# Padded rows in the raw tiles and state transfers in four pieces: a one-core RWKV kernel

## Chip, cores and metric

One Trainium2 chip; the kernel runs on 1 of its cores. The metric is the device time of one execution in microseconds, lower is better. The time before is a median of 317.09 us over 3 runs (315.88 to 317.64).

## What is computed

The WKV recurrence of RWKV over k and v of shape (16, 2048, 256), float32, with a decay vector w and a bonus vector u of 256 numbers. Each of the 16 x 256 channels carries three numbers (aa, bb, pp) through 2048 steps:

```python
for b in range(batch):
    aa, bb, pp = 0, 0, -1e38                 # vectors of d_model
    for t in range(seq_len):
        kk, vv = k[b, t, :], v[b, t, :]
        ww = u + kk
        qq = np.maximum(pp, ww)
        e1, e2 = np.exp(pp - qq), np.exp(ww - qq)
        output[b, t, :] = (e1 * aa + e2 * vv) / (e1 * bb + e2 + 1e-08)
        ww = pp - w + kk
        qq = np.maximum(ww, kk)
        e1, e2 = np.exp(ww - qq), np.exp(kk - qq)
        aa, bb, pp = e1 * aa + e2 * vv, e1 * bb + e2, qq
```

## The kernel before

**Tiles and stages.** Time is cut into 16 chunks of 128 steps, and each chunk into 4 tiles of 4 batches, so there are 64 tiles n; tile n belongs to chunk c = n // 4. A raw tile of k or v holds 128 time steps on the partitions and 4 batches x 256 channels behind each other (512 KB, 4 KB per partition). `load_k` and `load_v` (L91 to L102) fetch them: those of the first two tiles are issued on SP's queue, the other 124 on POOL's, where issuing is work of POOL itself (the rows L94 and L101). In HBM the four rows of 1 KB of one partition lie far apart, in the raw tile they lie side by side.

**One tile's way.** `round_k` (L184) rounds k to float32r, three of four tiles on DVE and the fourth on POOL; `cast_v` (L204) turns v into bfloat16, the first nine tiles on DVE, later ones on POOL. Twice per tile, PE forms sums of k over time in PSUM (`rows`, L191, and `logs`, L197), and ACT takes their exponentials into the ring EZR (`exps`, L200), which has room for 12 tiles. DVE multiplies them by v (`times_v`, L209), and PE sums (`sums`, L235). Ten tiles later the output is made: PE applies triangular matrices to EZR for the denominator (`den`, the name DEN) and the numerator (`num`, the name NUM), both in `apply` (L319); ACT takes logarithm and inverse (L337, L341); DVE multiplies (`mult`, L349) into one of five output buffers `ot`, and SP stores it in three DMAs (L355 and twice L358).

**State.** After the fourth tile of a chunk the state of all channels is carried on: sums are copied and turned (L241, L248), a chain of small DVE and ACT steps (L252 to L290) gives the state at the chunk's start, PE turns it back (`turn_back`, L294), DVE copies it to the 128 x 128 tile `cb` (L298), and `inject` (L305) writes it by DMA into EZR. There, rows 63 and 127 of EZR (each half chunk's last row) take the state, in place of the exponentials that stood there. DEN and NUM of the chunk's four tiles wait for this transfer ("IN"). The last chunk does without it.

**Order.** Every engine runs its instructions in the order of the program. That order is made when the program is built: each operation has a place (the table P, in units of a tile), operations are sorted by place, and the first whose predecessors are done and whose buffers are free is issued next (L409 to L439). The buffer counts stand in one line:

```python
NK, NKP, NV, NVB, NRD, NOT = 3, 5, 6, 2, 2, 5
```

`kf` has 5 buffers (NKP), `vr` 6 (NV; it also holds k of the first two tiles), `ot` 5 (NOT). SP's queue holds the state transfers and the stores, in program order; a transfer that waits for `cb` holds up the stores behind it. In each round of 4 tiles SP issues 2 state DMAs and 12 store DMAs. `zeros` (L135) issues matmuls that fill idle time of PE and change nothing.

Of the kernel before, what the change touches and what calls it, by code (L numbers as in the profile page):

```python
# [7 lines left out]
F32 = mybir.dt.float32  # L8
# [7 lines left out]
def kernel(  # L16
# [9 lines left out]
    K = tc.keep_in_program_order  # L26
    PE, DVE, SC, POOL, SP = nc.tensor, nc.vector, nc.scalar, nc.gpsimd, nc.sync

    B, T, Dm = k.shape
    HS = 64  # L30
    TC = 2 * HS
    NST = T // TC
    D = 2 * Dm
# [3 lines left out]
    BYSP = 2  # L37
    EARLY = 9
    PLAN = "DDDP"
# [2 lines left out]
    CAP = 54.0  # L42
    BIG = 1e30
    MM = 15
    FILL = 1
    P = {"LK": -5.73, "LV": -3.92, "RK": [-1.335, -1.2, -1.16, -1.575], "L": [-11.28, -6.145],
         "X": [-7.455, -4.505], "CV": [-0.72, -1.04, -0.995, -4.145], "TV": [1.435, 2.275, 2.29, 2.405],
# [10 lines left out]
    kppool = ctx.enter_context(tc.tile_pool(name="kppool", bufs=NKP))  # L58
    vpool = ctx.enter_context(tc.tile_pool(name="vpool", bufs=NV))
# [22 lines left out]
    def rows_of(x, n):  # L82
        c, p = divmod(n, 4)
        return x[4 * p:4 * p + 4, c * TC:(c + 1) * TC, :].rearrange("n t d -> t n d")

    KR, VR, VB = {}, {}, {}

    def how(n):
        return "D" if n < BYSP else PLAN[n % len(PLAN)]

    def load_k(n):  # L91
        if how(n) != "C":
            KR[n] = (vpool if n < BYSP else kppool).tile([128, 4, Dm], F32, tag="vr" if n < BYSP else "kf", name="kf")
            K((SP if n < BYSP else POOL).dma_start(out=KR[n], in_=rows_of(k, n)))  # L94
        else:
            KR[n] = kpool.tile([128, 4, Dm], F32R, tag="kr", name="kr")
            K(POOL.dma_start(out=KR[n], in_=rows_of(k, n)))

    def load_v(n):
        vr = vpool.tile([128, 4, Dm], F32, tag="vr", name="vr")  # L100
        K((SP if n < BYSP else POOL).dma_start(out=vr, in_=rows_of(v, n)))  # L101
        VR[n] = vr  # L102

# [5 lines left out]

    K(DVE.memset(WUf, 0.0))  # L110
    load_k(0)
    row_wu(w, 0)
    row_wu(u, 1)
# [19 lines left out]
    def zeros(m, first=False):  # L133
        for j in range(m):
            K(PE.matmul(TOT[:, 256:448], Z[:, 0:128], Z, start=first, stop=True, skip_group_check=True))  # L135
# [38 lines left out]
    EZR = consts.tile([128, 4, RING, 2, D], BF16, tag="EZR", name="EZR")  # L174
# [7 lines left out]
    def round_k(n):  # L182
        kr = kpool.tile([128, 4, Dm], F32R, tag="kr", name="kr")
        K((DVE if how(n) == "D" else POOL).tensor_copy(kr, KR[n]))  # L184
        KR[n] = kr
# [95 lines left out]
    def state_spread(c):  # L281
        CB, G = CB_of[c % 2], G_of[c % 2]
        x = AB[:, :, :, 0:2].rearrange("p a (b m) h -> p a h b m", b=4)
        y = G[:, 2, :, 1:3].rearrange("p (b m) h -> p h b m", b=4).unsqueeze(1).broadcast_to([128, 2, 2, 4, 8])
        if c >= MM:
            x, y = (z.rearrange("p a h b m -> p h a b m") for z in (x, y))
# [14 lines left out]
    def inject(c):  # L301
        cb = st.pop((c, "cb"))
        r0 = 4 * c % RING
        for q in (1, 0):
            K(SP.dma_start(out=EZR[HS - 1::HS, 2 * (1 - q), r0:r0 + 4, :, :].rearrange("h p i (b x) -> h (p i b) x", b=4),  # L305
                           in_=cb[HS * q:HS * q + HS, :]))


    RD, NUM, OT = {}, {}, {}
# [1 line left out]
    def apply(out_tile, n, names, q0):  # L311
        c, p = divmod(n, 4)
        if c >= MM:
            names = ({"L": "S", "LN": "SN"}[names[0]], names[1])
        for s in range(2):
            for i in range(2):
                for h in range(2):
# [3 lines left out]
                                tile_position=(r, o), skip_group_check=True))  # L321
        if c >= MM:
            for b in range(4):
# [40 lines left out]
    def step(name, place, fn, args=(), after=(), take=None, give=(), mode=0):  # L364
        ops[name] = dict(place=place, fn=fn, args=args, after=list(after), take=take, give=give, mode=mode)

    for n in range(NP):
# [4 lines left out]
        tail = n >= NP - LAG  # L372
        place = lambda key: m + (P["TAIL"][key] + (n - NP + LAG) * P["TAIL"]["step"] if tail else P["OUT"][key][j])
        kb = "V" if early else "KP" if how(n) != "C" else "K"
        if n:
            step(("LK", n), n + P["LK"], load_k, (n,), [("LK", n - 1)], kb)
        else:
            free["V"] -= 1
        step(("LV", n), n + P["LV"], load_v, (n,), [("LV", n - 1)] + ([("LK", n)] if n else []), "V")
        if how(n) != "C":  # L380
            step(("RK", n), put("RK"), round_k, (n,), [("LK", n), ("RK", n - 1)], "K", [kb])
# [8 lines left out]
        if j == 3:  # L390
            s = P["STATE"][0 if c == 0 else 2 if c == NST - 1 else 1]
            for i, (name, fn, *after) in enumerate((
                    ("CS", copy_sums, ("S", n)), ("TU", turn, ("CS", c), ("CH", c - 1)), ("SL", state_logs, ("TU", c)),
                    ("FR", state_frames, ("SL", c), ("SN", c - 1)), ("OF", state_offsets, ("FR", c)),
                    ("SW", state_weights, ("OF", c)), ("CH", state_chain, ("SW", c), ("KP", c - 1)),
                    ("SS", state_spread, ("CH", c)), ("TK", turn_back, ("SS", c), "mats"), ("BK", copy_back, ("TK", c)),
                    ("IN", inject, ("BK", c)), ("SN", state_next, ("OF", c)), ("KP", state_keep, ("CH", c)))):
                if not (name in ("SN", "KP") and c + 1 == NST or name == "IN" and c >= MM):
                    step((name, c), n + s[i], fn, (c,), after, mode=1)
# [12 lines left out]
    while todo:  # L412
        for name in todo:
            o = ops[name]
# [13 lines left out]
        if o["give"] == ["X"]:  # L428
            x = held[("DEN", name[1]) if name[0] == "LN" else ("R",) + name[1:]]
# [5 lines left out]
        if o["mode"] and not quiet:  # L435
            zeros(P["Z0" if name[-1] < FILL else "Z"].get(name[0], 0))
        quiet = quiet and name[0] != "CS" or name[0] == "S" and name[1] % 4 == 3
# [32 lines left out]
```

## Time and profile before

| | |
|---|---|
| median of 3 runs | 317.09 us |
| profiled execution | 316.14 us |
| its span, first to last instruction | 314.4 us |
| mean granted TensorE clock | 0.971 |
| HBM read, written | 67.12 MB, 33.55 MB |
| L200 exponentials, ACT | 128 of 1.01 us |
| L337 and L341, ACT | 64 of 1.02 us and 64 of 1.06 us |
| L349 output multiplication, DVE | 64 of 1.22 us |
| L184 rounding of k | 48 of 0.73 us on DVE, 16 of 1.04 us on POOL |
| L204 cast of v | 9 of 0.73 us on DVE, 55 of 1.28 us on POOL |
| L94, L101 issue of a load, POOL | 62 of 0.76 us, 62 of 0.78 us |
| a load from issue to landing | 7.8 us (k), 8.1 us (v), median |

Busy shares are averages over the span, over stages with different limits. Idle time of an engine counts only where that engine, or one that waits for it, sets the end. The time of a load's issue on POOL is not the time of its transfer: the transfer runs on the 16 DMA engines, which all queues share. A packet record of the trace is one piece of a transfer on one DMA engine, with its queue (q0: issued by POOL; q1: issued by SP), start, duration and size.

### The profile page before, as it was taken

The page shows a single profiled execution, that of the slowest core. Times are in us where ns is not written, and L with a number is a line of the kernel's source. Part 1 is how long each engine was busy: PE and PEld are TensorE (multiplying, and loading weights), DVE is VectorE, ACT ScalarE, POOL GpSimd, SP SyncE. Part 2 cuts the span into 40 slices and gives each one's busy share as a digit, 9 for nine tenths or more (in the row PEclk, how much of TensorE's full clock was granted, in tenths as well). Part 3 has the DMA queues.
Part 4 walks back from the last instruction along what each step waited for, and adds up shares of the span by engine and source line. Part 5 has one row for each costly group of instructions (what it writes and reads, how often), then busy time and mean ns, then how long its engine had stood idle before and what let it go on. Part 6 is the DMA issues. An engine that isn't in the chain of part 4 may idle for free.

```text
span 314.4 us, 7474 instructions
## 1 busy us (share of the span) xinstructions
PE 275.7 (88%) x2927; PEld 127.2 (40%) x2927; DVE 242.9 (77%) x430; ACT 259.1 (82%) x289; POOL 181.7 (58%) x213
## 2 busy tenths in 40 slices
PE   7898977999998998999897999799998979987840
PEld 7444742444343443444343434334443434432430
DVE  5879874588887879898878688787887866898650
ACT  1585554999999998999897999789998977997960
POOL 8855582385868585777848486846767552510000
PEclk9999997999999999999999999989999998999995
DMA  7999999889999999999999999999999996636986
GB/s 233 353 347 347 350 346 323 253 247 344 315 354 380 378 377 353 384 374 389 346 394 371 384 345 371 383 356 358 331 391 361 394 321 226 176 98 182 270 252 176
DMA packets 57840, 101.67 MB, mean 323 GB/s; under 512 B 7108, under 2 KB 41932, under 8 KB 57804
## 3 DMA queue, kind: packets, MB, share of 16 engines
q0 software_dynamic: 17856, 65.02, 59.0%
q1 hardware_dynamic: 39932, 36.16, 35.9%
q8 instruction: 23, 0.38, 0.5%
q14 instruction: 13, 0.11, 0.1%
q10 hardware_dynamic: 16, 0.01, 0.0%
HBM read 67.12 MB, written 33.55 MB: 320 GB/s over the span
## 4 chain that ended last, share of the span: by engine, by line
DMA 41%; PE 26%; ACT 12%; DVE 11%; issue 4%; SPq 3%; DVEq 0%; ACTq 0%
DMA out_dram<-ot 33%; ACT EZR L200 7%; DVE ot L349 7%; PE X L197 6%; DMA EZR<-cb 6%; PE TOT L135 5%; PE X L191 4%; PE num L319 3%; PE X L319 3%; ACT rd L337 3%; SPq L358 2%; PE TOT L235 2%; DMA WUf<-in_u_dram 2%; ACT rd L341 2%; DVE EZR L209 1%
## 5 line engine op out<-in xcount | busy, mean ns | idle before, releaser
L200 ACT ACTIVATE EZR<-X 128x1024 bf16<-128x1024 f32 x128 | 125.2, 1014 | 21.1 <-PE X L197 21.1
L349 DVE TENSOR_TENSOR ot<-num,rd 128x1024 f32<-128x1024 f32 x64 | 78.0, 1219 | 28.6 <-DMA out_dram<-ot 8.2
L94 POOL DMA_DIRECT2D kf<-in_k_dram x62 | 47.1, 760 | 72.3 <-DVE kr L184 66.3
L204 POOL CAST vb<-vr 128x1024 bf16<-128x1024 f32 x55 | 70.2, 1277 | 21.1 <-DVE EZR L209 19.0
L209 DVE TENSOR_TENSOR EZR<-EZR,vb 128x2048 bf16<-128x2048 bf16 x64 | 79.6, 1262 | 0.9 <-ACT EZR L200 0.9
L337 ACT ACTIVATE rd<-X 128x1024 f32<-128x1024 f32 x64 | 65.4, 1023 | 12.5 <-PE X L319 12.1
L341 ACT ACTIVATE rd<-rd 128x1024 f32<-128x1024 f32 x64 | 67.8, 1059 | 2.0
L135 PE MATMUL TOT<-Z 128*128 128x192 bf16 x367 | 64.8, 261 | 2.2 <-DVE Z L119 1.6
L191 PE MATMUL X<-WU,CO 64*64 64x512 bf16 x512 | 53.4, 406 | 1.8 <-DVE WU L166 0.9
L135 PEld LDWEIGHTS <-Z 128*128 128x128 bf16 x367 | 33.8, 102 | 50.5 <-issue 48.4
L101 POOL DMA_DIRECT2D vr<-in_v_dram x62 | 48.3, 779 | 2.1 <-DMA vr<-in_v_dram 1.8
L197 PE MATMUL X<-kr,NLE 128*128 128x512 f32 x128 | 46.9, 448 | 0.0
L197 PE MATMUL X<-kr,NLZ 128*128 128x512 f32 x128 | 46.2, 442 | 0.0
L184 DVE CAST kr<-kf 128x1024 fp32r<-128x1024 f32 x48 | 35.1, 732 | 1.7 <-PE X L197 0.9
L319 PE MATMUL num<-EZR,LN 64*64 64x512 bf16 x240 | 25.0, 406 | 12.3 <-DVE ot L349 9.2
L319 PE MATMUL X<-EZR,L 64*64 64x512 bf16 x240 | 24.8, 401 | 8.6 <-DMA EZR<-cb 6.6
L191 PEld LDWEIGHTS <-CO 64*64 64x64 bf16 x512 | 15.9, 104 | 37.8 <-issue 35.8
L319 PE MATMUL num<-EZR,IdN 64*64 64x512 bf16 x256 | 25.7, 384 | 0.0
L319 PE MATMUL X<-EZR,Id 64*64 64x512 bf16 x256 | 25.6, 380 | 0.0
L235 PE MATMUL TOT<-EZR,OH 128*32 128x256 bf16 x512 | 24.0, 281 | 0.9 <-DVE EZR L209 0.8
L298 DVE CAST cb<-TURN 128x128 bf16<-128x128 f32 x16 | 4.7, 291 | 22.6 <-PE TURN L294 22.6
L319 PEld LDWEIGHTS <-LN 64*64 64x64 bf16 x240 | 8.3, 104 | 34.0 <-issue 25.6
(70 smaller groups left out, 215.9 us busy)
## 6 DMA issues: line engine op xcount, KB each, us to landing
kf<-in_k_dram POOLq DMA_DIRECT2D x62, 512.0 KB, 7.8
vr<-in_v_dram POOLq DMA_DIRECT2D x62, 512.0 KB, 8.1
out_dram<-ot SPq DMA_DIRECT2D x64, 256.0 KB
out_dram<-ot SPq DMA_DIRECT2D x128, 128.0 KB
kf<-in_k_dram SPq DMA_DIRECT2D x2, 512.0 KB
vr<-in_v_dram SPq DMA_DIRECT2D x2, 512.0 KB
EZR<-cb SPq DMA_DIRECT2D x30, 16.0 KB
WUf<-in_w_dram ACTq DMA_DIRECT2D x1, 4.0 KB
```

The lines of the kernel that those rows point to most:

```text
L94: K((SP if n < BYSP else POOL).dma_start(out=KR[n], in_=rows_of(k, n)))
L101: K((SP if n < BYSP else POOL).dma_start(out=vr, in_=rows_of(v, n)))
L135: K(PE.matmul(TOT[:, 256:448], Z[:, 0:128], Z, start=first, stop=True, skip_group_check=True))
L191: K(PE.matmul(X[a][o:o + HS, i, :].rearrange("p (n d) -> p n d", n=2), CO[r:r + HS, q, :], WU[r:r + HS, :].unsqueeze(1).broadcast_to([HS, ...
L197: K(PE.matmul(X[a][:, i, :], (NLE, NLZ)[q], km[:, i, :], start=False, stop=True, skip_group_check=True))
L200: K(SC.activation(ez(n)[:, q], X[a], ACT.Exp))
L204: K((DVE if n < EARLY else POOL).tensor_copy(vb, VR.pop(n)))
L209: K(DVE.tensor_mul(ez(n)[:, 2:4], ez(n)[:, 0:2], vb.unsqueeze(1).broadcast_to([128, 2, 2, D])))
L319: K(PE.matmul(out_tile[o:o + HS, i, :], mats[names[s]][r:r + HS, r:r + HS], ez(n)[r:r + HS, q0 + s, i, :], start=s == 0, stop=s == 1, tile ...
L337: K(SC.activation(rd, X[a], ACT.Ln, scale=RS))
L341: K(SC.activation(RD[n], RD[n], ACT.Exp, scale=-1.0))
L349: K(DVE.tensor_mul(o.rearrange("p (i n) d -> p i (n d)", i=2), NUM.pop(n), RD.pop(n)))
```

## The change

Two edits. First, `raw` allocates the raw tiles of k and v with 8 more floats (32 B) behind each row of 256 and hands out the view without them, so that the rows of a partition stand 1056 B apart instead of 1024. The rounding and the cast read through that view. Second, a state transfer is issued as four DMAs instead of two. Before, each wrote 32 rows of `cb` (256 B each) into partition 63 and 32 into partition 127; now each piece moves 32 rows of `cb` into one partition, 8 KB in one run there. The order of the halves q stays. `CF` is 0, so `how` gives what it gave.

```diff
+    CF = 0
+    PAD = 8
...
     def how(n):
-        return "D" if n < BYSP else PLAN[n % len(PLAN)]
+        return "D" if n < BYSP else "C" if n < CF else PLAN[n % len(PLAN)]
+
+    def raw(pool, tag):
+        return pool.tile([128, 4, Dm + PAD], F32, tag=tag, name=tag)[:, :, 0:Dm]
 
     def load_k(n):
         if how(n) != "C":
-            KR[n] = (vpool if n < BYSP else kppool).tile([128, 4, Dm], F32, tag="vr" if n < BYSP else "kf", name="kf")
+            KR[n] = raw(vpool, "vr") if n < BYSP else raw(kppool, "kf")
             K((SP if n < BYSP else POOL).dma_start(out=KR[n], in_=rows_of(k, n)))
...
     def load_v(n):
-        vr = vpool.tile([128, 4, Dm], F32, tag="vr", name="vr")
+        vr = raw(vpool, "vr")
         K((SP if n < BYSP else POOL).dma_start(out=vr, in_=rows_of(v, n)))
...
         for q in (1, 0):
-            K(SP.dma_start(out=EZR[HS - 1::HS, 2 * (1 - q), r0:r0 + 4, :, :].rearrange("h p i (b x) -> h (p i b) x", b=4),
-                           in_=cb[HS * q:HS * q + HS, :]))
+            for h in range(2):
+                r, x = HS * h + HS - 1, 32 * (2 * q + h)
+                K(SP.dma_start(
+                    out=EZR[r:r + 1, 2 * (1 - q), r0:r0 + 4, :, :].rearrange("o p i (b x) -> o (p i b) x", b=4),
+                    in_=cb[x:x + 32, :]))
```

## The prediction

> **What bounds the kernel now.** I read the page first (busy shares, slices, queues), then the table by stage, the list of waits, the queue's own waits, and the timeline around the longest waits. All sums are made against the profiled execution: 316.14 us, of which 314.4 us are the span, so 1.7 us lie around it. The median of the runs shown is 317.09 us, 0.95 us above it.
>
> ```profile
> PE 275.7 (88%) x2927; PEld 127.2 (40%) x2927; DVE 242.9 (77%) x430; ACT 259.1 (82%) x289; POOL 181.7 (58%) x213
> ...
> q0 software_dynamic: 17856, 65.02, 59.0%
> q1 hardware_dynamic: 39932, 36.16, 35.9%
> ```
>
> The two DMA queues together hold the 16 engines for 95% of the span. PE's share contains idle-filling matmuls (L135, 64.8 us), so ACT, not PE, is the fullest compute engine. The table by stage shows when this holds (columns: PE, PEld, DVE, ACT, POOL busy us of 15, granted clock, DMA share, GB/s):
>
> ```profile
> 45.00:60.00 15.00, 10.51 (x100) 4.32 (x99) 7.01 (x16) 8.40 (x10) 7.00 (x9) 0.89 0.99 314
> ...
> 105.00:120.00 15.00, 13.26 (x148) 5.72 (x143) 11.32 (x20) 14.32 (x16) 10.60 (x12) 1.00 1.04 373
> 120.00:135.00 15.00, 14.88 (x158) 6.63 (x151) 12.85 (x21) 14.04 (x16) 9.94 (x11) 1.00 1.04 380
> ...
> 270.00:285.00 15.00, 13.30 (x163) 5.57 (x163) 13.17 (x23) 13.89 (x16) 4.98 (x4) 1.00 0.55 161
> ```
>
> From 75 to 255 us ACT is busy 12.0 to 14.6 of 15 us, mostly over 14, and the DMA engines are full at once: two limits of nearly the same height. Over those twelve rows ACT is idle 11.3 us. From 45 to 60 us ACT loses 6.6 us at one place:
>
> ```profile
> 39.34 1.24 SPq L305 DMA_DIRECT2D EZR<-cb  x2
> ...
> 49.36 0.41 PE L319 MATMUL X<-EZR,L 64*64 64x512 bf16 x4 [4.36 <-DMA EZR<-cb]
> ...
> 50.04 1.02 ACT L337 ACTIVATE rd<-X 128x1024 f32<-128x1024 f32 x1 [5.30 <-PE X L319]
> ```
>
> The first state transfer needs 10.0 us from its issue until DEN(0) may read it. PE has nothing else in its order from 45.0 us on, and ACT stands behind PE. The other waits that the change can touch:
>
> ```profile
> POOL kf L94 <- DVE kr L184: 66.3, 37, 6.7
> ...
> ACT rd L337 <- PE X L319: 12.1, 14, 5.3
> ...
> DVE ot L349 <- DMA out_dram<-ot: 8.2, 5, 2.5
> PE X L319 <- DMA EZR<-cb: 6.6, 4, 4.4
> ...
> PE num L319 <- DMA EZR<-cb: 2.4, 2, 1.4
> ```
>
> The first line is slack: loads wait for a free k buffer, and between 85 and 255 us a k tile lands 11 to 16 us before its rounding starts. Stores have no slack: DVE waits for an output buffer that a store holds, and SP itself is held, since the trace shows its 226 DMAs using eight completion semaphores in turn, each issue waiting for the landing of the eighth DMA before it:
>
> ```profile
> SPq L358 <- DMA out_dram<-ot: 18.3, 25, 1.6
> ```
>
> **Why the transfer is slow.** The trace's packet records tell it. Queue q1 closes its DMAs with 4 B packets: 3196 = 196 x 16 + 30 x 2, so every load and store runs on 16 engines and each state transfer on two. Loads on q0 move in packets of 4096 B, 192 ns each while only loads run, 172 to 188 ns beside stores. Between 43.8 and 47.9 us each of the two engines sends one 256 B packet (18 ns), then one 4096 B packet, every 207 ns: strict turns. The two transfers queue 64 such packets on each of those engines. At 267.8 us, with no load running, the first packet starts 1.19 us after the issue and the last 2.33 us; in the first transfer these are 4.47 and 9.25 us.
>
> **Part 1, four pieces of 32 rows.** It adds 30 SP issues of 0.6 us (L305, two in 1.2 us). If a piece spreads over 16 engines, an engine gets 2 packets of each piece, 8 per state instead of 64. The last piece is issued 3 x 0.62 = 1.9 us after the first, at 41.2 us. With the same 4.47 us to the first packet, two turns of 0.21 and the 0.8 us that lay between last packet and PE, it lands near 46.9 us: 2.5 us gained. The upper end is the whole 4.36 us of PE's wait, since DEN(0) can't start before 45.0. I take 3.5, because part 2 should shorten the turns too. Of the later waits on EZR<-cb (6.6 + 2.4 - 4.36 = 4.6 us) and ACT's one long wait behind them (2.53 us at 205 us) I take 2.5, bounds 0 and 4.6.
>
> What it costs: after each transfer twelve stores stand behind it on SP and start 1.2 us later, and the pieces take four of the eight semaphores instead of two. Stores already leave 6 to 10 us after their multiplication, and OT has five buffers, so this is hidden except where an output buffer is waited for: 5 waits x 1.2 = 6 us at most, nothing at least. I take 1.
>
> The Trainium skill, "DMA: Bandwidth & Descriptors", section on why a DMA increments its semaphore by 16, says that the engine count is the largest number up to 16 that divides the slowest dimension above 1 on both sides. Two destination rows give two engines there, as the 30 x 2 closing packets agree, and 32 rows against 32 would give 16. By it the piece spreads as assumed.
>
> **Part 2, the padding.** The destination of one partition's four rows is no longer one run of 4096 B. If packets follow runs, q0 goes from 15,872 packets of 4096 B to 63,488 of 1024 B. Price per KB: q1's 1 KB packets take 46 to 47 ns as stores beside loads; SP's four opening loads, the same shape in 1 KB packets, take 46 to 51, and move 350 GB/s from 5.4 to 8.4 us, against 346 GB/s for the 4096 B packets that follow. So the load-bound start (8 to 40 us) loses nothing. Beside stores a KB costs 43 to 47 ns now (172/4 to 188/4); 44 to 46 is +8 us of DMA time over the load phase (63,488 x 2 ns / 16), and 44 to 51 is +28. Cover: the 11 to 16 us of lead of the loads, and, on the two engines that carry the state now, the loss of 960 state packets each (960 x 18 ns = 17 us). I take 0, bounds -4 and +14 (28 less 14).
>
> The gain is in the turns. A tile's stores are 32 packets per engine: with a load packet between each, 32 x (46 + 176) = 7.1 us now, 32 x (46 + 48) = 3.0 us after. Stores land 8 us after issue on average and held DVE for 8.2 us. Bounds 0 and 8.2; I take 2, since ACT's idle time in those rows is shared with part 1's 2.5 and some 0.26 us per state step remains anyway.
>
> L94 and L101 on POOL (124 x 0.77 us): four times the destination runs. No row has a POOL issue of another shape; SP issues 512-packet loads in 0.45 to 0.51 us and 128-packet stores in 0.62, no growth with count. Bounds 0 and a doubling (+95 us of POOL, 277 of 314). I take 0. The casts (L184, L204) read rows with a gap; the elements stay side by side within 256. Nearest dearer row: DVE's one element per cycle in L349, 1219 against 732 ns, 57 x 0.49 = 28 us more DVE, mostly under ACT. I take 0, bounds 0 and +8.
>
> A rule against this part: the Trainium skill, "DMA: Bandwidth & Descriptors", section on how a descriptor splits into AXI transactions, has 256 B lines, and a run that starts off such a line pays for the part before it. Rows at +0, +32, +64, +96 B would then cost 32 to 35 beats instead of 32, an estimate of 5% on the loads, 0.05 x 184 = 9 us of DMA time. No row here shows an unaligned run.
>
> **Sum.** -3.5 - 2.5 + 1 - 2 = -7.0 us: span 307.4, profiled time 309.1, median 310.0 us.
>
> **Rivals.**
> 1. *The padding does not change the packets.* For: POOL's issue already names 1024 B elements, and packets may be filled to 4096 B whatever the runs. Then only part 1 acts: -2.5 - 2 + 1 = -3.5, 313.5 us.
> 2. *Slower: the finer packets overfill the DMA engines.* Place: 75 to 255 us. With 1.50 us of stores (512 x 47 / 16) and a share of 1.04, a tile fits ACT's 4.27 us (2 x 1.01 + 1.02 + 1.06, and a quarter of 0.28 + 0.36) as long as a load packet costs under 46 ns (1024 x 46 / 16 = 2.94; 4.44 / 1.04 = 4.27). At 51 ns a tile takes 4.58, 0.31 over, x 42 tiles = 13 us; at 53, 0.43 x 42 = 18. The lead of 12 us hides part, but stores now hold half the turns and loads come late first: PE X L197 then waits for kr. Net +3 to +14, 320 to 331; I put it at 325. For: the shares of 1.04. Against: the 350 GB/s of the opening loads.
> 3. *Slower: POOL's issue grows* to 1.5 us or more, delaying casts and loads: some 335.
> 4. *The pieces do not spread*, all 128 rows on one engine: 128 turns of 0.21 instead of 64, or stores held by the semaphores: +2 to +6, 321.
> 5. *The wait moves*: PE's freed time is given back at the output buffers: 316 to 317.5.
>
> **How the numbers follow.** Forecast 41%, rival 1 20%, rival 5 10%, rival 2 16%, rival 3 6%, rival 4 7%. About 0.5% (1.6 us) is what a measurement of this kernel can tell from no change. Faster: 0.41 x 0.95 + 0.20 x 0.85 = 0.56; slower: 0.29 from rivals 2 to 4 plus 0.02 of the others; same: the rest, 0.13. The forecast's own range is 304 to 315. Reaching out to most of rivals 2 and 4 gives 303 to 324, with about 5% below and 14% above.
>
> **What would show it.** Right: q0 with about 65,000 packets; closing packets of state pieces 16 each; EZR<-cb landing within 7 us of the first issue and PE's 4.36 us wait under 2; store landings shorter and DVE ot's wait on out_dram under 4 us; POOL's issue still near 0.75 us, the casts near 732 and 1277 ns. Wrong: q0 with 17,856 packets (rival 1); DVE kr or PE X waiting for DMA kf (rival 2); POOL busy well over 200 us (rival 3).

## The result and the profile after

The changed kernel takes 324.76 us (median of 4 runs, 323.81 to 326.19) against 316.49 us for the kernel before in the same comparison: ratio 1.031, 95% interval 1.025 to 1.038. It is slower by 8 us, where a gain of 7 us, to 310.0, was forecast; the measured median lies just above the range of 303 to 324. The profiled execution took 324.53 us, its span 322.8 us. Medians are over all runs of a kernel; ratios compare the undisturbed, fast runs of both kernels, so the quotient of two medians can differ from the ratio beside it.

Part 3 of the page after, the DMA queues (packets, MB, share of 16 engines):

```profile
q0 software_dynamic: 17856, 65.02, 58.7%
q1 hardware_dynamic: 40832, 36.16, 35.4%
```

q0 has the same 17,856 packets as before. The padding cut nothing: each packet still carries four rows of 1 KB, now to four separate places. q1 has 900 packets more. Its closing packets of 4 B are now 4096 = 196 x 16 + 60 x 16, so every piece of a state transfer did spread over 16 engines.

The timeline at the first state transfer, and ACT's instruction behind it:

```profile
38.87 2.53 SPq L312 DMA_DIRECT2D EZR<-cb  x4
...
44.98 0.40 PE L327 MATMUL X<-EZR,L 64*64 64x512 bf16 x1 [0.45 <-DMA EZR<-cb]
...
46.61 1.02 ACT L345 ACTIVATE rd<-X 128x1024 f32<-128x1024 f32 x1 [2.33 <-PE X L327]
```

Here the change does what it was expected to do: 6.1 us from the first issue to the first matmul of DEN(0) instead of 10.0, and ACT waits 2.33 us instead of 5.30. That matmul needs the first piece only. By the semaphore records (the trace's list of the moments at which a DMA reports a landed part) the four pieces land at 44.94, 45.91, 47.29 and 47.81 us; the whole transfer takes 8.9 us instead of 10.6, and ACT starts 3.4 us earlier, at 46.61 instead of 50.04. The multiplication of tile 8 starts at 83.3 us instead of 87.4: the kernel is 4 us ahead. The table by stage shows where it loses them and 8 more (columns as before):

```profile
45.00:60.00 15.00, 13.93 (x149) 5.93 (x150) 10.40 (x19) 12.41 (x14) 7.87 (x10) 1.00 0.99 332
...
105.00:120.00 15.00, 14.67 (x160) 6.43 (x159) 12.58 (x21) 14.65 (x18) 11.69 (x13) 1.00 1.04 356
120.00:135.00 15.00, 11.93 (x122) 5.07 (x120) 10.01 (x16) 11.21 (x14) 9.53 (x11) 0.99 1.02 363
...
180.00:195.00 15.00, 12.63 (x126) 5.20 (x123) 11.56 (x22) 11.22 (x14) 9.37 (x10) 0.89 0.98 327
...
255.00:270.00 15.00, 11.42 (x117) 4.54 (x112) 10.29 (x19) 9.97 (x13) 7.18 (x7) 0.89 0.99 338
```

Stretches in which ACT is full stand beside stretches in which it loses 4 to 5 us of 15. The list of waits after names two reasons, both DMAs of SP; the second fence is from the list of SP's own waits:

```profile
ACT rd L345 <- PE X L327: 23.5, 14, 4.8
DVE ot L357 <- DMA out_dram<-ot: 23.0, 9, 5.1
...
PE X L327 <- DMA EZR<-cb: 16.4, 9, 3.9
```

```profile
SPq L366 <- DMA out_dram<-ot: 22.9, 15, 3.0
...
SPq L363 <- DMA out_dram<-ot: 7.8, 8, 2.6
```

DVE's wait for an output buffer went from 8.2 to 23.0 us, and PE's wait for transfers from 6.6 to 16.4 us although the first one shrank. SP waits 30.7 us for stores to land before it may issue further stores (18.3 + 5.2 us before). That sum alone is no measure of the loss: it is 26.0 us in e1 and 20.1 us in e3 below, which lose more. What tells the kernels apart is where the waits fall. Added up from the issue and semaphore records of chunks 1 to 13, the first four stores behind each transfer wait 7.0 us in all for landings before and 25.7 us after, the most of it in chunks 3, 5, 7, 8, 10 and 12.

**One chunk, read side by side.** At 215 us both kernels happen to issue the transfer of chunk 10 at nearly the same time; it is the chunk with the longest of these waits. SP's queue before:

```profile
214.59 1.20 SPq L305 DMA_DIRECT2D EZR<-cb  x2
215.84 0.53 SPq L355 DMA_DIRECT2D out_dram<-ot  x1
216.42 1.32 SPq L358 DMA_DIRECT2D out_dram<-ot  x2
217.79 0.60 SPq L355 DMA_DIRECT2D out_dram<-ot  x1
```

and after:

```profile
209.81 1.75 SPq L366 DMA_DIRECT2D out_dram<-ot  x2
215.18 2.48 SPq L312 DMA_DIRECT2D EZR<-cb  x4
217.70 0.58 SPq L363 DMA_DIRECT2D out_dram<-ot  x1
220.64 2.40 SPq L366 DMA_DIRECT2D out_dram<-ot  x2
225.61 0.38 SPq L363 DMA_DIRECT2D out_dram<-ot  x1
```

The stores of tile 35 and the first of tile 36 start at 217.7, 220.6, 222.4 and 225.6 us instead of 215.8, 216.4, 217.1 and 217.8. The semaphore records of the trace say why. SP's DMAs use eight semaphores in turn, so an issue waits for the landing of the eighth DMA before it. With two transfer DMAs in between, the first store of tile 36 waits for the first store of tile 34, which landed at 217.12; with four in between it waits for the last store of tile 34, which landed at 225.59, and is issued 0.02 us later. The same window of the timeline after shows who stands behind that:

```profile
225.72 1.22 DVE L357 TENSOR_TENSOR ot<-num,rd 128x1024 f32<-128x1024 f32 x1 [5.14 <-DMA out_dram<-ot]
...
225.81 0.81 PE L327 MATMUL X<-EZR,L 64*64 64x512 bf16 x4 [3.86 <-DMA EZR<-cb]
227.08 1.02 ACT L345 ACTIVATE rd<-X 128x1024 f32<-128x1024 f32 x1 [4.79 <-PE X L327]
```

DVE waits for that same store of tile 34, whose output buffer it needs. The first piece of the transfer lands at 225.76, 0.17 us after the store, and the fourth at 226.28. The stores ahead of it had been issued 2 to 3 us later than before as well (the last at 210.8 against 207.9 us), and the last of them landed 5.6 us later.

### The profile page after: what moved, and what is told of

Same layout as the page of the kernel before. It is cut to its first block, busy times and chain, and to the rows that moved or that the text cites. A ratio compares the mean times of both kernels' runs of the same rounds, so it can differ in the third digit from the quotient of the medians.

```text
span 322.8 us, 7507 instructions
## 1 busy us (share of the span) xinstructions
PE 279.4 (87%) x2927; PEld 128.2 (40%) x2927; DVE 242.9 (75%) x430; ACT 258.3 (80%) x289; POOL 181.6 (56%) x213
## 3 DMA queue, kind: packets, MB, share of 16 engines
q0 software_dynamic: 17856, 65.02, 58.7%
## 4 chain that ended last, share of the span: by engine, by line
DMA 31%; PE 31%; ACT 22%; issue 6%; DVE 5%; SPq 3%; POOL 0%; DVEq 0%; POOLq 0%
DMA EZR<-cb 16%; ACT EZR L205 11%; DMA out_dram<-ot 9%; PE X L202 7%; ACT rd L345 7%; DMA kf<-in_k_dram 6%; PE TOT L140 5%; PE X L327 5%; PE X L196 5%; PE num L327 4%; ACT rd L349 3%; DVE ot L357 3%; PE TOT L240 2%; SPq L366 2%; PE TURN L253 1%
## 5 line engine op out<-in xcount | busy, mean ns | idle before, releaser
L202 PE MATMUL X<-kr,NLE 128*128 128x512 f32 x128 | 47.9, 456 | 0.0
L327 PE MATMUL X<-EZR,L 64*64 64x512 bf16 x240 | 26.8, 400 | 18.8 <-DMA EZR<-cb 16.4
L189 DVE CAST kr<-kf 128x1024 fp32r<-128x1024 f32 x46 | 33.8, 734 | 1.4 <-DMA kf<-in_k_dram 1.4
L327 PE MATMUL num<-EZR,LN 64*64 64x512 bf16 x240 | 26.1, 408 | 5.2 <-DVE ot L357 3.8
L327 PE MATMUL X<-EZR,Id 64*64 64x512 bf16 x256 | 27.0, 380 | 0.0
L327 PE MATMUL num<-EZR,IdN 64*64 64x512 bf16 x256 | 26.9, 390 | 0.0
L202 PEld LDWEIGHTS X<-kr,NLE 128*128 128x128 f32 x128 | 20.6, 202 | 3.4 <-issue 3.2
```

The source lines that it names most:

```text
L202: K(PE.matmul(X[a][:, i, :], (NLE, NLZ)[q], km[:, i, :], start=False, stop=True, skip_group_check=True))
L327: K(PE.matmul(out_tile[o:o + HS, i, :], mats[names[s]][r:r + HS, r:r + HS], ez(n)[r:r + HS, q0 + s, i, :], start=s == 0, stop=s == 1, tile ...
```

## The experiments

Ratios are to the kernel before, run on the same chip in the same rounds, with 95% intervals. DMAs per chunk are those on SP.

| kernel | SP DMAs a chunk | median us, kernel before us | ratio |
|---|---|---|---|
| both edits | 16 | 324.76, 316.49 | 1.031 [1.025, 1.038] |
| e1 pieces only | 16 | 326.5, 315.55 | 1.036 [1.030, 1.042] |
| e2 padding only | 14 | 314.32, 315.55 | 0.995 [0.989, 1.000] |
| e3 two more DMAs behind the transfer | 16 | 331.98, 315.07 | 1.056 [1.046, 1.066] |
| e7 two more ahead of it | 16 | 322.54, 313.52 | 1.027 [1.015, 1.039] |
| e6 pieces, fewer stores | 14 | 317.26, 315.07 | 1.005 [0.999, 1.010] |
| e10 before, fewer stores | 12 | 313.67, 317.21 | 0.983 [0.972, 0.995] |
| e4 padding, pieces in chunk 0 alone | 14 | 310.96, 315.07 | 0.984 [0.971, 0.997] |
| e5 transfers on POOL | 12 | 307.16, 315.07 | 0.977 [0.966, 0.988] |
| e9 four pieces on POOL | 12 | 307.38, 313.52 | 0.983 [0.977, 0.988] |
| e8 pieces in chunk 0, then POOL | 12 | 303.35, 313.52 | 0.968 [0.962, 0.975] |

**The two edits apart (e1, e2).**

```diff
-    PAD = 8
+    PAD = 0
```

> Four pieces, no padding. The changed kernel showed 17,856 packets of 4096 B on q0 as before, so the padding did not cut the packets. Theory A (the four pieces cause the loss: on all 16 engines they stand behind every store that SP issued before, and they hold four of the eight semaphores): slower by 2 to 4%, 322 to 329 us, with PE X L-matmuls waiting 10 us or more for EZR<-cb as in the changed kernel (16.4 us). Theory B (the padding causes the loss, by slower 4096 B packets beside stores): faster than before, 310 to 315 us, with the first wait cut and the later ones under 5 us in sum.

For e2 the padding stays and `inject` is that of the kernel before.

> Padding alone, two-piece transfers. Theory A: within 0.7% of before, 314 to 319 us, the first wait of 4.4 us on EZR<-cb as before. Theory B: slower by 2 to 4%, 322 to 329 us, q0 packets of 178 to 209 ns beside stores instead of 171 to 188.

Theory A held, theory B fell: the whole loss comes with the four pieces. The padding alone is worth 0 to 1%. One of the ten runs of e2 took 752.58 us, for a reason that is not known; the ratio does not count it. In e1 the first four stores behind each transfer wait 23.1 us in all for landings, in e2 3.2 us.

**The count, with the transfer unspread (e3).** The transfer stays as before, on two engines, and two DMAs of 256 B follow it:

```diff
             K(SP.dma_start(out=EZR[HS - 1::HS, ...], in_=cb[HS * q:HS * q + HS, :]))
+        for j in range(2):
+            K(SP.dma_start(out=SCR[j:j + 1, :], in_=cb[j:j + 1, :]))
```

> The kernel before (no padding, two-piece transfers on two engines) plus two DMAs of one 256 B row on SP behind each transfer, into a scratch tile that nobody reads. So 16 DMAs a chunk as with four pieces, and nothing spread. Count theory (two more DMAs a chunk on SP: eight semaphores cover two fewer stores, and 1.2 us of issue): slower by 2 to 4%, 322 to 329 us, DVE ot waiting over 15 us for stores. Spread theory (the pieces lose because all 16 engines carry them behind the stores): within 1% of before, 313 to 319 us.

With almost no bytes added the kernel loses 5.6%, more than the four pieces cost. The waits of e3:

```profile
DVE ot L353 <- DMA out_dram<-ot: 20.9, 10, 4.2
...
PE X L323 <- DMA EZR<-cb: 10.0, 6, 4.4
```

DVE's wait for stores appears as in the changed kernel, and the state transfer is not spread here. The first four stores behind the two DMAs wait 18.6 us in all for landings, against 7.0 before. The count theory was too low with 2 to 4%: these DMAs bring no shorter first wait to set against the loss. The run is no test without any spread, though: q1 shows 480 packets of 16 B and 480 closing packets more than before, 30 x 16 of each, so each extra DMA itself ran on 16 engines and held its semaphore until the slowest of them had landed. Two more DMAs on one or two engines were not tried.

**Pieces at the old count (e6).** Four pieces, but two tiles of each chunk store their second half in one DMA (the halves of 64 steps stand exchanged in the output; the bytes are the same):

```diff
+        if p % 2:
+            K(SP.dma_start(out=out[4 * p + 2:4 * p + 4, c * TC:(c + 1) * TC, :].rearrange("n t d -> t n d"), in_=o[:, 2:4, :]))
+            return
         for h in range(2):
```

> Four pieces, no padding; of every second tile the second half of the output goes out in one DMA instead of two, the same bytes, with its two half chunks of 64 steps exchanged in the output. So 14 DMAs a chunk as before, and the pieces still on 16 engines. Count theory: the loss is gone and the shorter first wait is left, 309 to 316 us. Spread theory: slower by 2 to 4% still, 322 to 329 us.

With the count back at 14 the loss is 0.5% instead of 3.6%. The first wait is short here too (0.41 us on PE), so some 1% of gain should have been left and was not: the median lies above the 309 to 316 us expected, and PE X waits 11.7 us for transfers, against 6.6 us before. So e6 does not clear the pieces. Fewer stores are a gain in themselves (e10 below, 0.983), and set against that the pieces still cost some 2% (1.005 / 0.983). Four of the eight semaphores are still held by pieces at one time, and the first four stores behind each transfer wait 28.9 us in all, no less than with 16 DMAs, while the kernel is faster than e1: that sum shows where SP is held, but it too does not give the loss by itself.

**Semaphore or issue time (e7).** As in e3, but the two extra DMAs read a constant and are issued ahead of the transfer, in time that SP spends waiting for `cb`:

```diff
+        for j in range(2):
+            K(SP.dma_start(out=SCR[j:j + 1, :], in_=Z[j:j + 1, 0:128]))
         for q in (1, 0):
```

> The kernel before plus two one-row DMAs per chunk on SP, this time from a constant tile and ahead of each transfer, where SP waits several us for cb anyway (109 us in all), so their 1.2 us of issue cost nothing. Semaphore theory (the two extra DMAs take two of the eight completion semaphores that the issues use in turn, so a store waits for the landing of a store two places later): still slower by 2% or more, 321 to 332 us. Issue-time theory (the stores start 1.2 us later): within 1% of before, 313 to 319 us.

Still slower by 2.7%: the 1.2 us of issue behind the transfer are not needed for the loss. The held semaphore is enough. These extra DMAs too ran on 16 engines (480 packets of 16 B). SP's own waits in e7 show it on the DMAs themselves:

```profile
SPq L309 <- DVE cb L298: 67.8, 12, 34.9
SPq L362 <- DMA out_dram<-ot: 20.4, 18, 2.6
...
SPq L309 <- DMA out_dram<-ot: 9.6, 6, 3.7
SPq L307 <- DMA out_dram<-ot: 5.5, 8, 1.6
```

L307 is the extra DMA, L309 the transfer; both now wait for stores to land, and at 12 of the 15 transfers SP still waits for `cb` behind the extra DMAs. The first four stores behind each transfer wait 19.9 us in all for landings. The 2.9% between e3 and e7 were not taken apart further; e3 adds the issue time ahead of twelve stores, and its extra DMAs land after the transfer.

**The other direction (e10).** The edit of e6 on the kernel before: 12 DMAs a chunk.

> The kernel before (two-piece transfers, no padding) with the second half of every second tile stored in one DMA instead of two, the same bytes, its two half chunks exchanged in the output: 12 DMAs a chunk. Semaphore theory: the kernel before is itself held by the count, so 14 to 12 gains where 14 to 16 lost; 306 to 313 us, DVE ot waiting under 5 us for stores. If only the pieces or their place matter: within 0.7% of before.

Faster by 1.7%, the median 0.7 us above what was expected; its four runs reach from 309.83 to 316.74 us, so the size is loose. The other half of the expectation was missed, in the profile of the run of 315.59 us:

```profile
DVE ot L349 <- DMA out_dram<-ot: 11.7, 6, 4.1
```

That is more than the 8.2 us before, not under 5. The times agree with the count theory (12, 14 and 16 DMAs a chunk give 0.983, 1 and 1.027 to 1.056), but this profile does not show through which wait two DMAs fewer gain.

**Keeping the gain (e4, e5, e9, e8).** e4 uses four pieces only for chunk 0, where no store runs yet:

```diff
         for q in (1, 0):
+            if c == 0:
             for h in range(2):
...
+            else:
+                K(SP.dma_start(out=EZR[HS - 1::HS, 2 * (1 - q), r0:r0 + 4, :, :].rearrange("h p i (b x) -> h (p i b) x", b=4),
+                               in_=cb[HS * q:HS * q + HS, :]))
```

> Padding, four pieces for chunk 0 alone, two-piece transfers after it. Both theories: the first wait falls from 3.2 to 4.4 us to about 0.5 us and nothing is lost later, so 2 to 4 us under the padding alone (314.3 us): 310 to 313 us.

PE's first wait is 0.37 us, and the median lies 3.4 us under that of the padding alone, as expected (the intervals of the two ratios overlap). e5 leaves out the pieces and the padding and issues the old two-piece transfers on POOL:

```diff
-            K(SP.dma_start(out=EZR[HS - 1::HS, ...
+            K(POOL.dma_start(out=EZR[HS - 1::HS, ...
```

> The kernel before with the two-piece transfers issued on POOL's queue: SP keeps 12 DMAs a chunk, all stores, and a transfer stands behind loads instead of stores. Count theory: SP issues stores earlier, DVE ot waits under 8 us for stores; 308 to 316 us if POOL's order does not suffer. Spread theory says nothing of it beyond that. Either way POOL waits for cb (SP did so for 109 us), and loads and casts stand behind it: slower, 318 to 330 us, if POOL has to wait more than a few us per chunk.

SP keeps its eight semaphores for stores, the median is 0.8 us below the range expected, and the wait of DVE falls as the count theory says:

```profile
DVE ot L349 <- DMA out_dram<-ot: 2.8, 3, 1.0
```

But e5 takes away more than two DMAs. In the kernel before SP stands and waits for `cb` before each transfer, with the stores behind it:

```profile
SPq L305 <- DVE cb L298: 109.3, 15, 36.4
```

A tile's first store is issued 6.2 us (median) after its multiplication there, and 8 to 11.6 us after it for the tiles right behind a transfer (3, 7, and so on to 51); in e5 the median is 0.03 us. e10 has the same 12 DMAs on SP but keeps this wait, and there it is 5.1 us. On POOL's queue the transfer also moves in other packets (4 of 4096 B in place of 64 of 256 B). Which of these makes the gain of e5 was not taken apart; in e5 SP still waits 30.9 us for stores to land.

e9 issues the four pieces on POOL:

> Four pieces without padding, all issued on POOL's queue, so the pieces are on 16 engines but SP's semaphores serve stores alone. Semaphore theory: no loss from the pieces, 304 to 312 us, DVE ot under 8 us behind stores. If the spread pieces were a loss in themselves: 318 us or more.

Away from SP the pieces cost nothing that can be told from e5, with DVE's wait at 1.8 us. e8 is e4 with the later transfers on POOL:

> Padding, chunk 0's transfer in four pieces on SP, every later transfer in two pieces on POOL's queue: the two gains seen so far together, 2.5 to 4 us for the first wait and 7 us for the transfers away from SP: 302 to 308 us. If they overlap, no better than the second alone, 306 to 309 us.

It is 3.2% under the kernel before, within the 302 to 308 us expected and the fastest version found. It has the padding too, which e5 has not, and the intervals of e8 and e5 overlap, so how much each part adds is not measured.

## Why the prediction was wrong

- **What bounds the kernel.** Right as far as it went: ACT is nearly full wherever nothing waits, and stores without slack hold the rest. The eight semaphores were named there, from the trace, but got no price.
- **Part 1, the first wait.** Right. 16 engines per piece, and ACT starts 3.4 us earlier where 3.5 were taken. DEN(0) starts at 44.98 us, since its first matmul needs one piece and not all four; the 46.9 worked out belongs to the last piece, which landed at 47.81. By 83 us 4 us are gained. The rule that the Trainium skill states for the number of engines ("DMA: Bandwidth & Descriptors", section on why a DMA increments its semaphore by 16) gives 16, and the 60 x 16 closing packets agree.
- **Part 1, the later waits on EZR<-cb.** Wrong sign: a gain of 2.5 us was taken; PE X's waits grew from 6.6 to 16.4 us. A transfer's landing was priced by its own packets, but in the side-by-side chunk it lands 0.17 us after the store ahead of it, so fewer packets per engine did not help there. In chunks 1 to 14 the first piece always landed behind the last of the stores just ahead of it, where the transfer on two engines had landed up to 1.7 us before that store in 5 of 14.
- **Part 1, the cost on SP.** This is the step that failed. It counted "5 waits x 1.2 = 6 us at most" and took 1, that is, it priced the issue time of two DMAs. It said that the pieces take four of the eight semaphores and gave that no price. The price is not an issue but a landing: a store waits for a DMA two places later in the order, and in the chunk shown a store starts up to 7.8 us later than before, part of it carried over from the chunks ahead. e7 shows 2.7% without the issue time, e3 5.6% with it, and DVE's wait went from 8.2 to 23.0 us; how much of the loss in the changed kernel is issue time is not measured. The cover named for it, that stores leave 6 to 10 us after their multiplication anyway, was no slack: most of that lag is time behind a transfer that waits for `cb` (with 12 DMAs a chunk on SP, e10 keeps 5.1 us of it, and e5, with the transfers away, 0.03), and an output buffer comes free only when its last store has landed, on average 16.7 us after its multiplication before and 18.0 us after (tiles 8 to 55).
- **Part 2, the padding.** Rival 1 was right that it doesn't do what it was taken to do: packets unchanged, so no shorter turns and no 2 us from them. POOL's issues stayed at 0.76 and 0.78 us and the casts at 0.73 and 1.28 us, as assumed. The Trainium skill's rule on runs off a 256 B line ("DMA: Bandwidth & Descriptors", section on how a descriptor splits into AXI transactions), from which an estimate of 9 us of DMA time was made, does not show here: e2 is not slower, and its load packets of 4096 B took 187 ns between 15 and 45 us, not more than the 192 ns before.
- **Rivals.** Rival 2 landed on the number (325 us) with the wrong mechanism: no packet became finer. Rival 4 named the mechanism, stores held by the semaphores, but gave it +2 to +6 us and 7%. The pieces alone cost 11 us (326.5 against 315.55), net of what the first wait brought. Rival 5 named the place, the output buffers, but only as a gain given back there.

## What to carry to other kernels

When a queue's issues share a fixed number of completion semaphores, count DMAs per round before splitting one: each extra DMA makes every following issue wait for a landing one place later, however few its bytes. A lag between "ready" and "issued" on a DMA queue is not yet slack: look at what the queue stands behind (here a transfer that waits for its source, and the landings of earlier DMAs) and at when the buffer has to come free. Splitting a latency-bound transfer pays where its queue is empty (here the first chunk), and moving it off the queue of the stores paid for the later ones (e5, e8, e9), by fewer held semaphores or by the shorter wait in front of the stores.

## What the runs showed of the hardware

- A load on POOL's queue moves in packets of 4096 B even when the four 1 KB rows of a packet go to places 1056 B apart; the same loads on SP's queue move in packets of 1024 B.
- Rows 32 B off did not slow the loads but sped them up a little where few other transfers run: of the 4096 B packets that start between 15 and 45 us, one takes 187.1 to 187.8 ns on average in the padded kernels (both edits, e2, e4, e8) and 191.8 to 192.6 ns in the eight unpadded ones. It was not looked for, and the reason is not known.
- A transfer on 16 engines, issued behind stores of the same queue, landed behind the last of them in all 14 later transfers of the changed kernel, at the least 0.17 us behind; on two engines, in the kernel before, its first half landed ahead of that store in 5 of 14, by up to 1.7 us. With no store in flight the first transfer had landed 8.9 us after its issue in four pieces and 10.6 us in two.
- A DMA of a single row of 256 B on SP's queue was moved as 16 packets of 16 B, on 16 engines (e3, e7): 480 such packets for 30 DMAs. Up to 13.2 us passed from its issue to its landing (e7).
